# The recurrent layer's output projection by quarters: seven products of 512 x 512 x 512 in place of eight

## The chip, the cores and the metric

The program runs on one core of a Trainium2 chip. The metric is the device time of one execution in microseconds (us); less is better. Engines are called PE (matmul), PEld (its weight load), DVE (vector), ACT (scalar), POOL (GpSimd) and SP (the queue that issues the transfers).

## What is computed

A trunk of two layers over 1024 tokens behind 16 learned meta tokens, 1024 wide: attention first, then the recurrent layer that is changed here. In the recurrent layer every channel runs a linear recurrence over the tokens, its result is multiplied by a gate, and the product is projected and added to the residual; a last norm follows, and the 16 meta tokens are dropped.

```
h = rmsnorm(x, b_norm_g);  u, gate = split(h @ b_w_in)
uc = causal_conv4(u);  r, i = sigmoid(uc @ w_rg + b_rg), sigmoid(uc @ w_ig + b_ig)   # 4 blocks of 256
a = exp(-8 r softplus(-lam));  hs[t] = a[t] hs[t-1] + sqrt(1 - a^2) (i uc)
y = hs * silu(gate)
out = rmsnorm(x + y @ b_w_out, final_norm_g)[16:]
```

All is float32. Each matrix product is made of three matmuls: both operands are split into a rounded high part (ACT copies it, `hi_of`) and the remainder (DVE subtracts, `lo_of`), and high x high, high x low and low x high are added in one accumulating bank (`mm3`, lines 85 to 88).

## The kernel before

The recurrent layer works by channel tile: 8 tiles `ct` of 128 channels, in 4 blocks of two. `b_u(ct)` makes the convolved input `uc` (bank names `pu`; three multiply-adds on DVE, L768) and its split `uh`, `ul`. `b_rec(blk, us)` makes the two gates of a block (banks `pz`, 72 matmuls of 348 or 344 columns that read `uh`, `ul` of both tiles), then on ACT sigmoid, exp, tanh and square root, and on DVE the recurrence as a scan (L813). `b_gate(ct)` makes `silu(gate)` (banks `pg`, 2 x 24 matmuls of 512 columns, sigmoid on ACT, product on DVE at L834) and leaves it in `Y[:, ct]`. `b_mul(ct)` multiplies `Y` by the scan's result: on POOL, for the last tile on DVE (L822). The table `gates` says which gates stand ahead of which block.

The projection then takes the 8 token tiles of 128 in turn. For each it splits `Y` (`yh_b`, `yl_b`), and for both halves of 512 output columns adds 8 x 3 matmuls in a bank `bo`, so 384 in all; the last tile's second half is cut in two pieces of 256 columns, which makes 408. DVE adds the bank to the residual row `h` (L887), ACT squares it (L888), and the norm follows (`rms_r`, L132 to L140; result `ot`, L899), then the store. The weights `wb` come in through a pool of four stage buffers of 512 KB (tag `stg`) and are split like the rest (L572).

Each engine works through its own queue in order. The order in the queues is not that of the code alone: the framework's scheduler places instructions by an estimate of its own, so a later step's instruction can stand ahead of an earlier step's. PSUM has 8 banks here: six under tag `m` (`ps_m`) and two under tag `t` (`ps_t`).

Of the kernel before, what the change touches and what calls it, by code (L numbers as in the profile page):

```python
# [62 lines left out]
def trunk(ctx, tc, x, meta, a_norm_g, a_w_in, a_q_g, a_kv_g, a_w_uq, a_w_ukv, a_w_out,  # L63
# [799 lines left out]


    st_w2, pw2 = open_pool("wo2", bufs=1)
    st_bo, pbo = open_pool("bo", bufs=2, side="right")
    g_f = pbo.tile([P, D], F32, name="g_f", bufs=1)
    nc.sync.dma_start(g_f, final_g.rearrange("(a d) -> a d", a=1).broadcast_to([P, D]))
    wb0b = load_wo(pw2, b_w_out, 0, "wb", 6, (2, 3))
    ws = [(wb0[0] + wb0b[0], wb0[1] + wb0b[1]), load_wo(pw2, b_w_out, 1, "wb", 6)]  # L870
    for i in range(SEQ // P):
# [24 lines left out]
        for half in range(2):
            c = slice(half * 512, (half + 1) * 512)
            if not last:
                nc.vector.scalar_tensor_tensor(ot[:, c], ht[:, c], r, g_f[:, c], ALU.mult, ALU.mult)  # L899
            elif half:  # L900
                nc.vector.tensor_scalar(ot[:, c], ot[:, c], r, None, ALU.mult)
            else:
                nc.scalar.activation(ot[:, c], ot[:, c], AF.Copy, scale=r)
# [45 lines left out]
```

## Time and profile before

| | us |
|---|---|
| median of 3 runs (lowest, highest) | 934.7 (933.69, 935.65) |
| the profiled execution's own time | 937.55 |
| its span, first to last instruction | 935.7 |
| PE busy, DVE busy, ACT busy, POOL busy | 904.4, 554.3, 458.0, 35.6 |
| mean granted PE clock, of full | 0.99 |

The profile is one execution; its rows count from the span's start. Matmuls overlap, so the time that a row gives for one is longer than the step from one to the next; the step is read from starts. On DVE and ACT too the next instruction starts a little before the row of the one ahead ends.

### The profile page before, as it was taken

Reading aid. Unit: us, or ns where it says so; the run is one execution under the profiler, and the core shown is the slowest. Engines: PE = TensorE matmul, PEld = TensorE weight load, DVE = VectorE, ACT = ScalarE, POOL = GpSimd, SP = SyncE. Lnnn points to the kernel's source line nnn. Section 1 sums busy time; section 2 is a strip of 40 time slices with the busy share of each in tenths; the row PEclk is TensorE's granted clock in tenths of the full one; section 3 lists DMA queues with packets and bytes.
Section 4 is the critical chain, followed back from the end, with each engine's and each line's share of the span. In section 5 each row is a group of like instructions: output and inputs, shape, how many; then the busy total and the mean of one; then the engine's idle time right before and its main releaser. Section 6 shows DMA issues by size and latency. Waiting matters only on the chain.

```text
span 935.7 us, 13771 instructions
## 1 busy us (share of the span) xinstructions
PE 904.4 (97%) x5351; PEld 831.5 (89%) x5351; DVE 554.3 (59%) x1188; ACT 458.0 (49%) x937; POOL 35.6 (4%) x38
## 2 busy tenths in 40 slices
...
DMA packets 68449, 67.02 MB, mean 72 GB/s; under 512 B 14896, under 2 KB 52528, under 8 KB 68384
## 3 DMA queue, kind: packets, MB, share of 16 engines
...
## 4 chain that ended last, share of the span: by engine, by line
PE 87%; ACT 5%; DVE 5%; DMA 2%; issue 2%; SPq 0%; ACTq 0%; DVEq 0%
PE pt L536 4%; PE ga L87 3%; PE ga L86 3%; PE ga L88 3%; PE bo L87 3%; PE ao L86 3%; PE bo L88 3%; PE ao L88 3%; PE bo L86 3%; PE ao L87 3%; PE pu L88 2%; PE pu L86 2%; PE pu L87 2%; PE s L491 2%; PE o L88 2%; PE o L87 2%
## 5 line engine op out<-in xcount | busy, mean ns | idle before, releaser
L509 ACT ACTIVATE p<-s,m 116x116 f32<-116x116 f32 (+4 forms) x80 | 55.4, 694 | 42.8 <-PE pt L536 15.2
L80 ACT ACTIVATE pth<-pt 116x348 fp32r<-116x348 f32 (+5 forms) x152 | 57.7, 397 | 29.3 <-PE pt L536 25.6
L83 DVE TENSOR_TENSOR ptl<-pt,pth 116x348 fp32r<-116x348 f32 (+5 forms) x152 | 64.0, 437 | 10.3 <-ACT pth L80 9.7
L88 PE MATMUL pu<-x2h,l_wu 128*128 128x348 f32 (+1 forms) x192 | 61.5, 321 | 0.4 <-DVE l_wu L83 0.4
L88 PE MATMUL ga<-xth,l_wg 128*128 128x348 f32 (+1 forms) x192 | 61.7, 321 | 0.0
L86 PE MATMUL pu<-x2h,h_wu 128*128 128x348 f32 (+1 forms) x192 | 61.7, 322 | 0.0
L87 PE MATMUL pu<-x2l,h_wu 128*128 128x348 f32 (+1 forms) x192 | 61.7, 321 | 0.0
L87 PE MATMUL ga<-xtl,h_wg 128*128 128x348 f32 (+1 forms) x192 | 61.6, 321 | 0.0
L86 PE MATMUL ga<-xth,h_wg 128*128 128x348 f32 (+1 forms) x192 | 61.5, 320 | 0.0
L501 DVE CUSTOM_DVE_ANT_0 s<-s,maskt 116x116 f32<-116x116 f32 (+8 forms) x72 | 49.4, 686 | 17.6 <-PE s L495 17.6
L536 PE MATMUL pt<-ident,p 116*116 116x116 f32 (+1 forms) x360 | 54.6, 263 | 2.3 <-DVE ptl L83 1.8
L87 PE MATMUL bo<-wbl,yh_b 128*128 128x512 f32 (+1 forms) x136 | 51.9, 383 | 1.3 <-DVE wbl L572 1.3
L86 PE MATMUL bo<-wbh,yh_b 128*128 128x512 f32 (+1 forms) x136 | 51.8, 383 | 1.1 <-ACT wbh L80 1.1
L86 PE MATMUL ao<-wah,yh_a 128*128 128x512 f32 x128 | 50.5, 396 | 1.7 <-ACT yh_a L80 1.1
L88 PE MATMUL bo<-wbh,yl_b 128*128 128x512 f32 (+1 forms) x136 | 51.2, 380 | 0.0
L87 PE MATMUL pg<-x2l,h_wbg 128*128 128x512 f32 x128 | 50.6, 395 | 0.0
L88 PE MATMUL pg<-x2h,l_wbg 128*128 128x512 f32 x128 | 50.3, 393 | 0.0
L88 PE MATMUL ao<-wah,yl_a 128*128 128x512 f32 x128 | 50.3, 394 | 0.0
L86 PE MATMUL pg<-x2h,h_wbg 128*128 128x512 f32 x128 | 50.2, 392 | 0.0
L87 PE MATMUL ao<-wal,yh_a 128*128 128x512 f32 x128 | 49.8, 391 | 0.0
L491 PE MATMUL s<-kh,qh 128*116 128x348 f32 (+7 forms) x120 | 42.1, 351 | 6.7 <-ACT p L509 6.7
L536 PEld LDWEIGHTS pt<-ident,p 116*116 116x116 f32 (+1 forms) x360 | 41.5, 135 | 5.9 <-DVE ptl L83 2.5
...
## 6 DMA issues: line engine op xcount, KB each, us to landing
wg<-in_a_w_in SPq DMA_DIRECT2D x8, 512.0 KB, 3.9
wa<-in_a_w_out SPq DMA_DIRECT2D x8, 512.0 KB, 3.5
wu<-in_b_w_in SPq DMA_DIRECT2D x8, 512.0 KB, 4.0
wbg<-in_b_w_in SPq DMA_DIRECT2D x8, 512.0 KB, 3.9
wb<-in_b_w_out SPq DMA_DIRECT2D x8, 512.0 KB, 3.9
h<-hscr SPq DMA_DIRECT2D x8, 512.0 KB, 3.9
...
x<-in_x SPq DMA_DIRECT2D x7, 512.0 KB, 3.3
```

Source lines behind the costliest of these rows:

```text
L80: nc.scalar.activation(dst, src, AF.Copy)
L83: nc.vector.tensor_tensor(dst, src, bc(hi), ALU.subtract)
L86: nc.tensor.matmul(ps, lh, rh, start=start, stop=False)
L87: nc.tensor.matmul(ps, lh, rl, start=False, stop=False)
L88: nc.tensor.matmul(ps, ll, rh, start=False, stop=stop)
L491: nc.tensor.matmul(ps, a, kth[:, k0:k0 + w], start=True, stop=False)
L501: MKD[h, t] = nc.vector.tensor_tensor_reduce(pv, pv, mk, 1.0, -NEG, ALU.add, ALU.min, m[:, s:s + 1])
L509: MK[h, t] = nc.scalar.activation(dst, pv, AF.Exp, bias=mx, scale=-1.0, accum_out=l[:, s:s + 1])
L536: nc.tensor.transpose(pv[:nk, j], p[:, k0:k0 + nk], ident[:n, :n])
```

## The change

The projection of `Y` (1024 tokens x 1024 channels) by `b_w_out` is written as a product of 2 x 2 quarters of 512, with seven products of quarters in place of eight (Strassen's way, with 15 sums, in Winograd's form). `a11`, `a12` are the first 512 tokens with channel tiles 0 to 3 and 4 to 7, `a21`, `a22` the second 512 tokens.

- Each product is 4 banks (128 tokens each) x 4 channel tiles x 3 matmuls of 512 columns: 48, so 336 in all. The products run in the order P1, P7, P2, P6, P5, P3, P4 (each named by the numbers of its operands, `w1` and `y1` to `w7` and `y7`). Banks `b2` stay in use through P1, P7, P6 and P4, `b1` holds P2, `b3` holds P5 and P3; the partial sums in a bank are read between products.
- Sums of `Y` quarters are 4 DVE instructions of 2048 elements per partition (L976, L993, L1007, L1008), in place in `Y`. Each product's left operand is split anew: one ACT and one DVE instruction of 2048 (L893, L894), for P1 two of 1024.
- Sums of weights are made by the transfer: a plain load on SP, then a load from POOL's queue that adds to what lies in the stage buffer (`accum_op`, L872). There are eight of these, of 512 KB. `wchain` takes W12, then + W22, + W11, + W21, and is split in between for P7, P6 and P4; `wt1` is W11 + W12. Each weight operand is split as before, 7 x 2 instructions of 1024 on ACT and on DVE.
- All 8 residual rows are loaded ahead (`hr`), in the space that `x2h`, `x2l` had until the last gate; a finished bank is added to, or taken from, one or two quarters of them (`upd`, L949 and L951, 512 columns, 36 times in place of 17). Square, norm and store follow for each token tile (`square`, `finish`); the last tile is no longer cut.
- Gate 6 moves ahead of the last block's recurrence (`gates`), and gate 7 stands alone behind it.

The line numbers of the rows below in `order` fences that are above 840 are those of the changed kernel.

```diff
@@ -82,10 +82,10 @@
     def lo_of(dst, src, hi):
         nc.vector.tensor_tensor(dst, src, bc(hi), ALU.subtract)
 
-    def mm3(ps, lh, ll, rh, rl, start, stop):
-        nc.tensor.matmul(ps, lh, rh, start=start, stop=False)
-        nc.tensor.matmul(ps, lh, rl, start=False, stop=False)
-        nc.tensor.matmul(ps, ll, rh, start=False, stop=stop)
+    def mm3(ps, lh, ll, rh, rl, start, stop, **kw):
+        nc.tensor.matmul(ps, lh, rh, start=start, stop=False, **kw)
+        nc.tensor.matmul(ps, lh, rl, start=False, stop=False, **kw)
...
-    gates = {0: [0], 1: [1, 2], 2: [3, 4], 3: [5]}
+    gates = {0: [0], 1: [1, 2], 2: [3, 4], 3: [5, 6]}
...
-    wb0 = load_wo(pw1, b_w_out, 0, "wb", 2, (0, 1))
-    for ct in (6, 7):
-        b_gate(ct)
-        gated.add(ct)
-        settle()
...
+    TI = SEQ // (2 * P)
+    def w_raw(name):
+        return [stage(f"{name}_{j}").rearrange("p (k c) -> p k c", k=2) for j in range(2)]
+    def w_load(raw, kq, nq, add=False):
+        for j in range(2):
+            r0 = kq * 512 + j * 2 * P
+            src = b_w_out[r0:r0 + 2 * P, nq * 512:(nq + 1) * 512].rearrange("(k p) c -> p k c", p=P)
+            if add:
+                nc.gpsimd.dma_start(raw[j], src, accum_op=ALU.add)
+            else:
+                nc.sync.dma_start(raw[j], src)
+    def w_split(raw, pool, name):
+        th, tl = ("wh", "wl") if pool is wpg else ("woh", "wol")
+        hs, ls = [], []
+        for j in range(2):
+            hi = pool.tile([P, 2, 512], F32R, name=f"h_{name}_{j}", tag=th, bufs=2)
+            lo = pool.tile([P, 2, 512], F32R, name=f"l_{name}_{j}", tag=tl, bufs=2)
+            hi_of(hi, raw[j])
+            lo_of(lo, raw[j], hi)
+            hs.append(hi)
+            ls.append(lo)
+        return hs, ls
+    def yq(cq, tq, t0=0, n=512):
+        c0 = NMETA + tq * 512 + t0
+        return Y[:, 4 * cq:4 * cq + 4, c0:c0 + n]
+    def y_split(yv, yh, yl, sign):
+        nc.scalar.activation(yh, yv, AF.Copy, scale=float(sign))
+        nc.vector.scalar_tensor_tensor(yl, yv, float(sign), bc(yh), ALU.mult, ALU.subtract)
+    def product(banks, w, ys, first):
+        for i in range(TI):
+            yh, yl, o = ys(i)
+            for k in range(4):
+                mm3(banks[i], yh[:, k, o:o + P], yl[:, k, o:o + P], w[0][k // 2][:, k % 2], w[1][k // 2][:, k % 2],
+                    first and k == 0, k == 3, skip_group_check=True)
+    g7 = gate_w(KT - 1)
+    r1 = w_raw("wq11")
+    w_load(r1, 0, 0)
+    w1 = w_split(r1, pw1, "wq11")
+    ra = w_raw("wchain")
+    w_load(ra, 0, 1)
+    b_gate(KT - 1, g7)
+    gated.add(KT - 1)
+    settle()
+    y1 = []
+    for j in range(2):
+        yh = pbw.tile([P, 4, 256], F32R, name=f"y1h{j}", tag=("up", "uh")[j], bufs=2)
+        yl = pbw.tile([P, 4, 256], F32R, name=f"y1l{j}", tag=("up", "ul")[j], bufs=2)
+        y_split(yq(0, 0, 256 * j, 256), yh, yl, -1)
+        y1.append((yh, yl))
+    w_load(ra, 1, 1, True)
+    b2 = [ps_m(f"b2_{i}") for i in range(TI)]
+    product(b2, w1, lambda i: (*y1[i // 2], (i % 2) * P), True)
...
+    hr = []
+    for i in range(2 * TI):
+        h_ = pbo.tile([P, D], F32, name=f"hr{i}", tag="hr", bufs=2 * TI)
         t0 = NMETA + i * P
-        ys = [y_half(wpg if i == 0 else pbo, j, t0, P, f"b{i}", 2) for j in range(2)]
-        ht = pbo.tile([P, D], F32, name=f"h2_{i}", tag="ht", bufs=3)
-        nc.sync.dma_start(ht, hscr[t0:t0 + P, :])
-        ot = pbo.tile([P, D], F32, name=f"ot{i}", tag="ot", bufs=2)
-        last = i == SEQ // P - 1
-        cuts = (0, 512, 768, 1024) if last else (0, 512, 1024)
-        pieces = list(zip(cuts, cuts[1:]))
-        ms = sml.tile([P, 3], F32, name=f"fms{i}", tag="ms2")[:, :len(pieces)]
-        junk = wpg.tile([P, D], F32, name=f"junkf{i}", tag="wh") if last else ot
-        for j, (c0, c1) in enumerate(pieces):
-            half, o = c0 // 512, c0 % 512
-            ps = ps_m(f"bo{j}_{i}")[:, :c1 - c0]
-            out_mm(ps, ys, *[[w[:, :, o:o + c1 - c0] for w in ww] for ww in ws[half]])
-            hv = ht[:, c0:c1]
-            nc.vector.tensor_tensor(hv, ps, hv, ALU.add)
-            nc.scalar.activation(junk[:, c0:c1], hv, AF.Square, scale=1.0 / 32.0, accum_out=ms[:, j:j + 1])
-            if last:
-                nc.vector.tensor_tensor(ot[:, c0:c1], hv, g_f[:, c0:c1], ALU.mult)
+        nc.sync.dma_start(h_, hscr[t0:t0 + P, :])
+        hr.append(h_)
...
+    def yc(yv, name, sign=1):
+        yh = pbo.tile([P, 4, 512], F32R, name=f"ych_{name}", tag="ych", bufs=2)
+        yl = pbo.tile([P, 4, 512], F32R, name=f"ycl_{name}", tag="ycl", bufs=2)
+        y_split(yv, yh, yl, sign)
+        return lambda i: (yh, yl, i * P)
...
+    def upd(bank, i, cols, op):
+        h_ = hr[i][:, cols]
+        if op is ALU.add:
+            nc.vector.tensor_tensor(h_, bank, h_, ALU.add)
+        else:
+            nc.vector.tensor_tensor(h_, h_, bank, ALU.subtract)
...
+    a11, a12, a21, a22 = yq(0, 0), yq(1, 0), yq(0, 1), yq(1, 1)
+    w7 = w_split(ra, wpg, "wt3")
+    nc.vector.tensor_tensor(a21, a21, a11, ALU.subtract)
+    y7 = yc(a21, "s3")
+    for i in range(TI):
+        upd(b2[i], i, LEFT, ALU.subtract)
+        upd(b2[i], i, RIGHT, ALU.add)
+    r2 = w_raw("wq21")
+    w_load(r2, 1, 0)
+    w_load(ra, 0, 0, True)
+    product(b2, w7, y7, False)
+    g_f = pfo.tile([P, D], F32, name="g_f", bufs=1)
+    nc.sync.dma_start(g_f, final_g.rearrange("(a d) -> a d", a=1).broadcast_to([P, D]))
+    w2 = w_split(r2, pw1, "wq21")
+    y2 = yc(a12, "a12")
+    for i in range(TI):
+        upd(b2[i], i, RIGHT, ALU.subtract)
+    nc.vector.tensor_tensor(a21, a22, a21, ALU.subtract)
+    r5 = w_raw("wt1")
+    w_load(r5, 0, 0)
+    b1 = other("b1")
+    product(b1, w2, y2, True)
+    w6 = w_split(ra, wpg, "wt2")
+    y6 = yc(a21, "s2")
+    w_load(r5, 0, 1, True)
+    w_load(ra, 1, 0, True)
+    for i in range(TI):
+        upd(b1[i], i, LEFT, ALU.add)
+        square(i, 0) if i < 2 else None
+    nc.vector.tensor_tensor(a11, a11, a21, ALU.subtract)
+    nc.vector.tensor_tensor(a12, a12, a21, ALU.subtract)
+    product(b2, w6, y6, False)
+    w5 = w_split(r5, pw1, "wt1")
+    y5 = yc(a11, "s1")
+    r3 = w_raw("wq22")
+    w_load(r3, 1, 1)
+    for i in range(TI):
+        upd(b2[i], i, RIGHT, ALU.add)
+        upd(b2[i], i + TI, RIGHT, ALU.add)
+    b3 = other("b3")
+    product(b3, w5, y5, True)
+    w3 = w_split(r3, wpg, "wq22")
+    y3 = yc(a12, "s4")
+    for i in range(TI):
+        upd(b3[i], i + TI, RIGHT, ALU.add)
+    product(b3, w3, y3, False)
+    w4 = w_split(ra, pw1, "wt4")
+    y4 = yc(a22, "a22", -1)
+    for i in range(TI):
+        upd(b3[i], i, RIGHT, ALU.add)
+        if i >= 2:
+            square(i, 0)
+        square(i, 1)
+        finish(i)
+    product(b2, w4, y4, False)
+    for i in range(TI):
+        square(i + TI, 1)
+        upd(b2[i], i + TI, LEFT, ALU.subtract)
+        square(i + TI, 0)
+        finish(i + TI)
```

PE, where the last block's recurrence matmuls start (`pz6`, `pz7`: blocks' gates for channel tiles 6 and 7; `uh7`, `ul7`: the second tile's convolved input); before:

```order
L88 MATMUL pg5_1_8302<-x2h_6171,l_wbg5_8272 128x512
L86 MATMUL pz6_0_0_8339<-uh6_8170,h_wri3_8334 128x348
L87 MATMUL pz6_0_0_8339<-ul6_8171,h_wri3_8334 128x348
L88 MATMUL pz6_0_0_8339<-uh6_8170,l_wri3_8335 128x348
L86 MATMUL pz6_0_1_8347<-uh6_8170,h_wri3_8334 128x348
L87 MATMUL pz6_0_1_8347<-ul6_8171,h_wri3_8334 128x348
L88 MATMUL pz6_0_1_8347<-uh6_8170,l_wri3_8335 128x348
L86 MATMUL pz6_0_2_8355<-uh6_8170,h_wri3_8334 128x344
L87 MATMUL pz6_0_2_8355<-ul6_8171,h_wri3_8334 128x344
L86 MATMUL pz6_0_0_8339<-uh7_8265,h_wri3_8334 128x348
L86 MATMUL pz6_0_1_8347<-uh7_8265,h_wri3_8334 128x348
L88 MATMUL pz6_0_2_8355<-uh6_8170,l_wri3_8335 128x344
```

and with the change:

```order
L88 MATMUL pg6_1_8362<-x2h_6171,l_wbg6_8332 128x512
L86 MATMUL pz6_0_0_8399<-uh6_8170,h_wri3_8394 128x348
L87 MATMUL pz6_0_0_8399<-ul6_8171,h_wri3_8394 128x348
L88 MATMUL pz6_0_0_8399<-uh6_8170,l_wri3_8395 128x348
L86 MATMUL pz6_0_0_8399<-uh7_8265,h_wri3_8394 128x348
L87 MATMUL pz6_0_0_8399<-ul7_8266,h_wri3_8394 128x348
```

The 48 matmuls of gate 6 (`pg6`) now stand between gate 5 (`pg5`) and these; before, gate 5 was followed at once by the recurrence, and the first ones that read `uh7` came ninth and tenth.

DVE, behind the last block's first scan (`z6`, `z7`: recurrence; `pg7`: gate 7; `wb`: projection weights); before:

```order
L812 TENSOR_TENSOR z7_1_8413<-z7_0_8388,z7_1_8413 128x1040
L83 TENSOR_TENSOR yl_b0_0_8640<-Y_1217,yh_b0_0_8639 128x512
L834 TENSOR_TENSOR Y_1217<-pg6_1_8501,Y_1217 128x512
L813 SCALAR_TENSOR_TENSOR z7_0_8388<-a7_8441,z7_1_8413 128x1040
L834 TENSOR_TENSOR Y_1217<-pg7_0_8536,Y_1217 128x512
L822 TENSOR_TENSOR Y_1217<-Y_1217,z7_0_8388 128x512
L83 TENSOR_TENSOR yl_b0_1_8644<-Y_1217,yh_b0_1_8643 128x512
L834 TENSOR_TENSOR Y_1217<-pg7_1_8563,Y_1217 128x512
L822 TENSOR_TENSOR Y_1217<-Y_1217,z7_0_8388 128x512
L572 TENSOR_TENSOR wbl0_2_8606<-wb0_2_8603,wbh0_2_8605 128x1024
```

and with the change (`b2_0` to `b2_3`: the four banks of P1; `hr`: residual rows; `ycl_s3`: low part of P7's left operand; `wt3`, `wq21`: right operands of P7 and P2):

```order
L812 TENSOR_TENSOR z7_1_8473<-z7_0_8448,z7_1_8473 128x1040
L837 TENSOR_TENSOR Y_1217<-pg7_1_8567,Y_1217 128x512
L951 TENSOR_TENSOR hr0_8667<-hr0_8667,b2_0_8606 128x512
L949 TENSOR_TENSOR hr0_8667<-b2_0_8606,hr0_8667 128x512
L894 SCALAR_TENSOR_TENSOR ycl_s3_8693<-Y_1217,ych_s3_8692 128x2048
L813 SCALAR_TENSOR_TENSOR z7_0_8448<-a7_8501,z7_1_8473 128x1040
L951 TENSOR_TENSOR hr1_8669<-hr1_8669,b2_1_8607 128x512
L949 TENSOR_TENSOR hr1_8669<-b2_1_8607,hr1_8669 128x512
L951 TENSOR_TENSOR hr2_8671<-hr2_8671,b2_2_8608 128x512
L949 TENSOR_TENSOR hr2_8671<-b2_2_8608,hr2_8671 128x512
L822 TENSOR_TENSOR Y_1217<-Y_1217,z7_0_8448 128x512 x2
L83 TENSOR_TENSOR l_wq21_0_8761<-wq21_0_8704,h_wq21_0_8760 128x1024
```

The reading of P1's banks, P7's operand and P2's weights now share DVE's queue with the second scan; behind these rows stand one more bank's update, the sum at L993 and the low part of P2's left operand (`ycl_a12`), of 2048 elements.

DVE at the end of the program; before, the last rows but the norm of the last tile:

```order
L140 SCALAR_TENSOR_TENSOR r_f6_9188<-r_f6_9188,t_f6_9189 128x1
L899 SCALAR_TENSOR_TENSOR ot6_9129<-h2_6_9127,r_f6_9188,g_f_8601 128x512 x2
L887 TENSOR_TENSOR h2_7_9207<-bo0_7_9212,h2_7_9207 128x512
L890 TENSOR_TENSOR ot7_9209<-h2_7_9207,g_f_8601 128x512
L887 TENSOR_TENSOR h2_7_9207<-bo1_7_9240,h2_7_9207 128x256
L890 TENSOR_TENSOR ot7_9209<-h2_7_9207,g_f_8601 128x256
L892 TENSOR_TENSOR fmt7_9296<-fms7_9210 128x1
L887 TENSOR_TENSOR h2_7_9207<-bo2_7_9268,h2_7_9207 128x256
L890 TENSOR_TENSOR ot7_9209<-h2_7_9207,g_f_8601 128x256
```

and with the change, from the third of the last product's four tiles:

```order
L951 TENSOR_TENSOR hr6_8679<-hr6_8679,b2_2_8608 128x512
L951 TENSOR_TENSOR hr7_8681<-hr7_8681,b2_3_8609 128x512
L966 TENSOR_TENSOR fmt4_9184<-fms4_9179 128x1
L133 TENSOR_SCALAR v_f4_9186<-fmt4_9184 128x1
L134 RECIPROCAL t_f4_9188<-t_f4_9188 128x1
L136 SCALAR_TENSOR_TENSOR r_f4_9187<-t_f4_9188,v_f4_9186 128x1
L966 TENSOR_TENSOR fmt5_9203<-fms5_9198 128x1
L140 SCALAR_TENSOR_TENSOR r_f4_9187<-r_f4_9187,t_f4_9188 128x1
L133 TENSOR_SCALAR v_f5_9205<-fmt5_9203 128x1
L970 SCALAR_TENSOR_TENSOR ot4_9180<-hr4_8675,r_f4_9187,g_f_8758 128x512 x2
```

Before, each tile's norm and output stand behind that tile's own bank. With the change both last banks' updates (`hr6`, `hr7`) stand ahead of the norm and output of token tiles 4 to 7, of which tile 4's are shown and the other three follow in the same way.

## Rows read from the trace of the kernel before

**Rows 1.** The page, part 1: busy time, share of the span, instructions.

```profile
PE 904.4 (97%) x5351; PEld 831.5 (89%) x5351; DVE 554.3 (59%) x1188; ACT 458.0 (49%) x937; POOL 35.6 (4%) x38
```

**Rows 2.** Busy time by stretch; the first row names the columns.

```profile
core 0: us, PE busy (x) PEld busy (x) DVE busy (x) ACT busy (x) POOL busy (x), PEclk, DMA share, GB/s
740.00:760.00 20.00, 20.00 (x104) 17.72 (x104) 8.26 (x9) 8.69 (x14) 2.69 (x3) 1.00 0.18 56
797.09:814.46 17.37, 14.65 (x74) 13.90 (x72) 7.89 (x7) 8.86 (x15) 2.56 (x2) 0.80 0.15 52
814.46:836.70 22.24, 22.24 (x99) 18.03 (x97) 14.53 (x13) 13.91 (x15) 4.20 (x2) 1.00 0.21 71
836.70:847.34 10.64, 8.31 (x29) 6.14 (x28) 9.79 (x13) 6.98 (x10) 1.18 (x1) 0.84 0.50 167
847.34:928.78 81.44, 81.40 (x382) 68.22 (x380) 37.13 (x83) 22.72 (x52) 0.00 (x0) 1.00 0.24 82
928.78:935.70 6.92, 0.00 (x0) 0.00 (x0) 2.19 (x8) 1.52 (x4) 0.00 (x0) 0.68 0.20 76
```

**Rows 3.** Timeline of PE, last block's recurrence: start, length, instruction, [idle before].

```profile
800.67 0.59 PE L86 MATMUL pz<-uh,h_wri 128*128 128x348 f32 x2 [2.17 <-ACT uh L80]
...
802.63 0.66 PE L87 MATMUL pz<-ul,h_wri 128*128 128x348 f32 x1 [0.56 <-DVE ul L83]
...
805.11 0.49 PE L87 MATMUL pz<-ul,h_wri 128*128 128x348 f32 x1
805.40 0.49 PE L88 MATMUL pz<-uh,l_wri 128*128 128x348 f32 x1
...
808.28 0.37 PE L86 MATMUL pz<-uh,h_wri 128*128 128x344 f32 x1
```

**Rows 4.** Timeline of PE, start of the projection.

```profile
840.66 0.50 PE L86 MATMUL bo<-wbh,yh_b 128*128 128x512 f32 x1 [1.07 <-ACT wbh L80]
842.42 0.75 PE L87 MATMUL bo<-wbl,yh_b 128*128 128x512 f32 x1 [1.26 <-DVE wbl L572]
```

**Rows 5.** Timeline of ACT, the first gate sigmoid behind the last block's square roots.

```profile
826.29 0.60 ACT L308 ACTIVATE Y<-pg 128x512 f32<-128x512 f32 x1
```

**Rows 6.** Groups by form, 780 to 936: count, busy us, mean ns, idle before.

```profile
L822 POOL TENSOR_TENSOR Y<-Y,z 128x512 f32<-128x512 f32 x6 | 12.3, 2060 | 78.2 <-DVE z L813 59.8 <-DVE Y L834 18.4
...
L887 DVE TENSOR_TENSOR h<-bo,h 128x512 f32<-128x512 f32 x15 | 10.4, 690 | 21.4 <-PE bo L88 17.3 <-issue 4.1
...
L813 DVE TENSOR_TENSOR_SCAN z<-a,z 128x1040 f32<-128x1040 f32 x4 | 9.3, 2316 | 0.1
...
L572 DVE TENSOR_TENSOR wbl<-wb,wbh 128x1024 fp32r<-128x1024 f32 x6 | 7.0, 1219 | 1.2 <-ACT wbh L80 1.2
...
L80 ACT ACTIVATE wbh<-wb 128x1024 fp32r<-128x1024 f32 x6 | 5.9, 1044 | 0.0
...
L812 DVE TENSOR_TENSOR z<-z,z 128x1040 f32<-128x1040 f32 x3 | 3.7, 1220 | 0.0
```

**Rows 7.** Timelines of POOL and DVE, where both work and where DVE works alone.

```profile
781.57 4.38 POOL L822 TENSOR_TENSOR Y<-Y,z 128x512 f32<-128x512 f32 x2 [34.22 <-DVE z L813]
...
782.48 2.32 DVE L83 TENSOR_TENSOR l_wbg<-wbg,h_wbg 128x1024 fp32r<-128x1024 f32 x1
...
841.15 4.62 DVE L572 TENSOR_TENSOR wbl<-wb,wbh 128x1024 fp32r<-128x1024 f32 x4
```

**Rows 8.** Timelines of DVE and SP's queue, the last two tiles' norms.

```profile
919.07 0.16 DVE L892 TENSOR_TENSOR fmt<-fms 128x1 f32<-128x1 f32 x1 [0.79 <-ACT ot L888]
...
920.24 1.41 DVE L899 SCALAR_TENSOR_TENSOR ot<-h,r_f,g_f 128x512 f32<-128x512 f32 x2
...
930.95 0.49 DVE L901 TENSOR_SCALAR ot<-ot,r_f 128x512 f32<-128x512 f32 x1
```

**Rows 9.** Transfers: count, KB each, median us from issue to landing.

```profile
wb<-in_b_w_out SPq DMA_DIRECT2D x8, 512.0 KB, 3.9
...
csk<-in_rope_k SPq DMA_DIRECT2D x1, 288.0 KB, 7.4
```

More of the change, by code (lines that the diff above doesn't have):

```diff
@@ L83, in lo_of @@
         nc.vector.tensor_tensor(dst, src, bc(hi), ALU.subtract)
-    def mm3(ps, lh, ll, rh, rl, start, stop):
-        nc.tensor.matmul(ps, lh, rh, start=start, stop=False)
-        nc.tensor.matmul(ps, lh, rl, start=False, stop=False)
-        nc.tensor.matmul(ps, ll, rh, start=False, stop=stop)
+    def mm3(ps, lh, ll, rh, rl, start, stop, **kw):
+        nc.tensor.matmul(ps, lh, rh, start=start, stop=False, **kw)
+        nc.tensor.matmul(ps, lh, rl, start=False, stop=False, **kw)
+        nc.tensor.matmul(ps, ll, rh, start=False, stop=stop, **kw)
     def mm_stack(ps, xp, k, n, wh, wl):
@@ L822, in b_mul, with gate_w, b_gate @@
             (nc.vector if ct == KT - 1 else nc.gpsimd).tensor_tensor(yv, yv, r[:, c0:c0 + 512], ALU.mult)
-    def b_gate(ct):
+    def gate_w(ct):
         raw = load_wcols(b_w_in, D + ct * P, KT, P, f"wbg{ct}")
-        wh, wl = split_page(raw, [P, KT, P], f"wbg{ct}")
+        return split_page(raw, [P, KT, P], f"wbg{ct}")
+    def b_gate(ct, pages=None):
+        wh, wl = pages or gate_w(ct)
         for c in range(2):
@@ L862, in trunk @@
     st_x2.close()
[L865 to L871, printed above, removed]
-        t0 = NMETA + i * P
-        ys = [y_half(wpg if i == 0 else pbo, j, t0, P, f"b{i}", 2) for j in range(2)]
-        ht = pbo.tile([P, D], F32, name=f"h2_{i}", tag="ht", bufs=3)
-        nc.sync.dma_start(ht, hscr[t0:t0 + P, :])
-        ot = pbo.tile([P, D], F32, name=f"ot{i}", tag="ot", bufs=2)
-        last = i == SEQ // P - 1
-        cuts = (0, 512, 768, 1024) if last else (0, 512, 1024)
-        pieces = list(zip(cuts, cuts[1:]))
-        ms = sml.tile([P, 3], F32, name=f"fms{i}", tag="ms2")[:, :len(pieces)]
-        junk = wpg.tile([P, D], F32, name=f"junkf{i}", tag="wh") if last else ot
-        for j, (c0, c1) in enumerate(pieces):
-            half, o = c0 // 512, c0 % 512
-            ps = ps_m(f"bo{j}_{i}")[:, :c1 - c0]
-            out_mm(ps, ys, *[[w[:, :, o:o + c1 - c0] for w in ww] for ww in ws[half]])
-            hv = ht[:, c0:c1]
-            nc.vector.tensor_tensor(hv, ps, hv, ALU.add)
-            nc.scalar.activation(junk[:, c0:c1], hv, AF.Square, scale=1.0 / 32.0, accum_out=ms[:, j:j + 1])
-            if last:
-                nc.vector.tensor_tensor(ot[:, c0:c1], hv, g_f[:, c0:c1], ALU.mult)
@@ new lines, in trunk @@
+    st_bo, pbo = open_pool("bo", bufs=2)
+    st_fo, pfo = open_pool("fo", bufs=2, side="right")
+    hr = []
+    for i in range(2 * TI):
+        h_ = pbo.tile([P, D], F32, name=f"hr{i}", tag="hr", bufs=2 * TI)
+        t0 = NMETA + i * P
+        nc.sync.dma_start(h_, hscr[t0:t0 + P, :])
[5 more added lines that the diff above has]
+        return lambda i: (yh, yl, i * P)
@@ new lines, in other, with square @@
+    def other(name):
+        return [(ps_m if i < 2 else ps_t)(f"{name}_{i}") for i in range(TI)]
+    LEFT, RIGHT = slice(0, 512), slice(512, 1024)
+    def upd(bank, i, cols, op):
[4 more added lines that the diff above has]
+            nc.vector.tensor_tensor(h_, h_, bank, ALU.subtract)
+    fms, junks = {}, {}
+    def square(i, half):
+        if i not in fms:
+            fms[i] = sml.tile([P, 2], F32, name=f"fms{i}", tag="ms2", bufs=2 * TI)
+            junks[i] = pfo.tile([P, D], F32, name=f"ot{i}", tag="ot", bufs=2)
+        c = slice(half * 512, half * 512 + 512)
+        nc.scalar.activation(junks[i][:, c], hr[i][:, c], AF.Square, scale=1.0 / 32.0,
+                             accum_out=fms[i][:, half:half + 1])
@@ L891, in trunk, with finish @@
+    def finish(i):
+        ot = junks[i]
         mt = sml.tile([P, 1], F32, name=f"fmt{i}", tag="ms")
-        nc.vector.tensor_tensor(mt, ms[:, 0:1], ms[:, 1:2], ALU.add)
-        if last:
-            nc.vector.tensor_tensor(mt, mt, ms[:, 2:3], ALU.add)
+        nc.vector.tensor_tensor(mt, fms[i][:, 0:1], fms[i][:, 1:2], ALU.add)
         r, _ = rms_r(mt, P, 1, f"f{i}")
```

10 lines of the change are left out of this document (2 added, 8 removed).

## The prediction

> **What bounds the kernel now.** I read the page's busy times first, then busy time by stretch over the last 140 us, then the timelines of the stretches in which PE was not busy, last the groups by form for prices. PE is busy 97% of the span and DVE 59% [rows 1], so work taken from PE pays at once as long as DVE, ACT and the transfers keep up, and PE's idle time is the other thing to look for. From 797 to the end there are three places of it [rows 2]. The last block's recurrence takes 17.37 us with PE busy for 14.65 at a granted clock of 0.80. The projection's first 10.64 us have 8.31 busy, clock 0.84. Behind the last matmul come 6.92 us of norm and store. The rest is packed: both gates (96 matmuls) take 22.24 us, 11.12 each, and the projection's main part 81.44 us for 332 matmuls of 512 columns and 48 of 256, as many columns as 356: 0.228 us for 512. All prices below are from this one execution; its own time is 937.55 for a span of 935.7, the median 934.7, and the sum is taken off each alike.
>
> **The recurrence: minus 6.0.** The ninth matmul waited 2.17 us for the copy of `uh7`, a later one 0.56 for `ul7` [rows 3]. After the first wait PE went at the lower of its two levels (1.2 GHz): steps of 0.29 us for 348 columns against (814.46 - 808.28) / 39 = 0.158 from 808.28 on [rows 2, 3]. Undisturbed, 72 matmuls take 11.3, so 6.0 are lost. With the change gate 6 stands in front, 11.12 us of PE work, and `uh7`, `ul7` are wanted only at 797.09 + 11.12 = 808.2. DVE has more to do before that: one stage slot serves gate 5's weights, `wq11_0` and `wq11_1` in turn. Gate 5's split ends at 784.80 [rows 7], a load lands 3.9 later [rows 9], copy and split take 1.04 and 1.22 [rows 6]: 791.2. One more multiply-add (1.2, as the 1040-wide rows), three ACT copies in a row (3.1) and a split bring gate 6's weights to about 796.8, just in time for 797.1; two more multiply-adds and splits bring `ul7` to 805 or 806. I take the whole 6.0; a load that lands later would take up to 1.5 of it. So the recurrence ends at 819.5, gate 7 at 830.7, where P1 starts (the old projection started at 836.7).
>
> **The matmuls: minus 11.2; the old start: minus 4.2.** 336 at 0.228 is 76.6. The old projection lasted 836.70 to 928.78, 92.08 us. In its first 10.64, 28 matmuls at 0.228 would have taken 6.4; the other 4.2 are two waits for weight splits (1.07 and 1.26) and the lower clock after them [rows 2, 4]. So 87.8 becomes 76.6, and the 4.2 go, since P1's weights and both its operands come early.
>
> **DVE at the start of the products: plus 4.6, and 1.0 for the clock.** The first sigmoid of the last gate ended 12.3 us behind the recurrence's last matmul (826.29 + 0.60 against 814.6) [rows 2, 5]; ACT now has one 1.0 us copy more in that chain, so it ends at 819.5 + 12.3 + 1.0, about 832.9. From there DVE's queue to the low part of P2's operand holds: 13 instructions of 512, 2 of 1040, 3 splits of 1024, 2 scans, 3 of 2048. Four splits in a row took 4.62, a step of 1.155, 0.065 under the mean of one [rows 6, 7]; I take that off each row: 13 x 0.62 + 2 x 1.155 + 3 x 1.155 + 2 x 2.25 + 3 x 2.2 = 25. The 2.2 is an estimate: 0.690 for 512 and 1.219 for 1024 [rows 6] make 2.28 for 2048 on a line. One of these meets tile 6's product on POOL, where a DVE instruction on two SBUF tiles took 2.32 instead of 1.22 [rows 7]: 1.1 more. Sum 26.1, done at 859.0. PE in that time has P1, three banks of P7, eight matmuls of P2 and P7's last bank: 104 x 0.228 = 23.7, done at 854.4. It waits 4.6 us in all, ahead of P7's first bank (low part, about 844.7), its second bank (two updates), and P2's remainder. Bounds: 3.5 without POOL, 8 if all three large ones are slowed. Waits of this size lowered the clock twice [rows 3, 4]; but while DVE is what PE waits for, a slower PE costs little, so 1.0, between 0 and rival A's 8.
>
> Behind that DVE just keeps up. During the rest of P2 and the first eight matmuls of P6 (48 x 0.228 = 10.9) it has three updates, two sums, a split and a low part, 9.6; for P5 and P3 about 9.5 and 9.4 against 10.9. The sum at L976 goes into DVE's queue two blocks earlier, where DVE is busy 8.26 us of 20 [rows 2]; without that gap it would cost its 2.2.
>
> **The transfers: 0.** No row shows an accumulating load. The nearest are plain ones: 3.9 us for 512 KB, at worst 7.4 for 288 KB in small pieces [rows 9]; I take 5, since these rows are 2 KB long like those of `wb`. The first is issued near 802.5 (gate 6's split, then a plain load) and wanted by ACT at 820.4, 18 us later; the tightest, `wt1`, near 855.5 (P2's split, then a plain load) and wanted at 866, when P2's reads release the split's buffers. Both ends fit. The rows `hr` start when gate 7 ends; even one after the other, `hr3` would land at 830.7 + 4 x 3.9 = 846.3, and is used at 852.
>
> The trace shows DVE and POOL slowing each other where both work, not one shut out [rows 7]. The Trainium skill's page SBUF — State Buffer, section SBUF: two separate sides, warns that a transfer issued by GpSimd starves while DVE holds their shared port, since GpSimd can't write its descriptors. That speaks against this change; its list names copies in the two-port mode, and its section Who interferes with whom leaves tensor-tensor work out, by inference. No row here shows it; by it the transfers would start late, which is rival B's case, near 935, and by the rows the sum stays.
>
> **The end: plus 8.0.** Before, only one tile's norm was left behind the last matmul. Now the updates of the last two banks stand ahead of the norms of tiles 4 to 7 on DVE, so four norms start when PE ends. One took 919.07 to 921.65, 2.58 with ACT's square root in between [rows 8]. One update 0.62, 4 x 2.58 = 10.3, and from the last DVE instruction (930.95 + 0.49) to the span's end 4.2, of which ACT's parallel half was done 0.2 later: 4.0. That is 14.9 against 6.92 [rows 2]; bounds 13.5 and 16.
>
> **The sum.** -6.0 - 11.2 - 4.2 + 4.6 + 1.0 + 8.0 = -7.8. Span 927.9, that execution 929.7, median 926.9.
>
> **The rivals.**
> A, the clock stays low through P7. Four waits within 15 us; the lower level lasted 7.6 us after 2.17 of idling [rows 3]. At 0.228 x 0.29 / 0.158 = 0.42, the 54 matmuls from 844.8 on take 22.6 and end at 867.4 instead of 859.0: 8.4, so 934. If P2's other 40 are slow too, 942. Against it: between the waits PE works without a gap, and the clock came back in such work.
> B, the other side: accumulating loads are slow, or begin late. Let one take T. The first holds up ACT's queue, and all behind it, by T - 18; `wt1` then holds up P5 by T - 10.5 - 3 (its split has about 3 to spare). At T = 20 that is 2 + 6.5, and the gain is gone; at 25 it is 18.5: 945. Against it: T would have to be 2.7 times the slowest load shown. For it: nothing here shows one.
> C, DVE is late in every product. Its rows add to some 72 us beside 76.6 of PE before the end, and P6 has 1.3 of margin. If one of 2048 takes 2.6, or POOL's transfers slow it as its products do, P2, P6 and the end lose 4 more: 931.
> D, less is lost: DVE's work of 2048 costs less than the line says and ACT's early squares let the last norms close up: waits 2, end 13, clock 0, so 922.
>
> **How the numbers follow.** Forecast 0.54 (its own range 924 to 930), A 0.13, B 0.11, C 0.14, D 0.08. 922 to 935 leaves out the slow ends of A and B and little below. About 0.2%, 1.9 us, can be told from no change here. Faster are the forecast, C, D and a little of A and B: 0.80. Same: the near ends of A and B, 0.07. Slower: their far ends, 0.13.
>
> **What would show it.** In the changed profile: no wait ahead of the first `pz` reading `uh7`, and 72 of them in about 11.4 us; P1 starting near 831; waits of PE between 841 and 860 ended by DVE (`ycl_s3`, `hr`, `ycl_a12`), some 5 us; no wait ended by a transfer of POOL's queue; about 15 us between PE's last matmul and the end, with DVE busy most of it. The forecast is wrong if loads of `wchain` or `wt1` end waits of ACT, if the clock's digit stays under 9 beyond one slice, or if PE waits for DVE after 870.

## The result, and the profile after

The changed kernel takes 928.6 us (median of 4 runs, 928.06 to 929.28); the kernel before, on the same chip, 934.3 (median of 4). The ratio is 0.9937, with a 95% interval of 0.992 to 0.9955: 5.9 us less, at least 4.2 and at most 7.5. The forecast was 926.9, its range 922 to 935. The profiled execution has an own time of 928.06 and a span of 926.3.

The page's first part, to be set against [rows 1]:

```profile
PE 888.9 (96%) x5279; PEld 816.0 (88%) x5279; DVE 584.7 (63%) x1206; ACT 466.3 (50%) x932; POOL 43.6 (5%) x46
```

PE has 15.5 us less, DVE 30 us more. Busy time by stretch shows where it went. The cuts are gates 5 and 6, the last block's recurrence, gate 7, P1, from P1's end to just behind P2's wait, the rest of the products, and what follows the last matmul:

```profile
core 0: us, PE busy (x) PEld busy (x) DVE busy (x) ACT busy (x) POOL busy (x), PEclk, DMA share, GB/s
784.65:806.89 22.24, 22.24 (x98) 18.03 (x97) 19.42 (x16) 11.73 (x15) 4.59 (x4) 1.00 0.50 122
806.89:818.27 11.38, 11.38 (x74) 11.38 (x72) 3.07 (x3) 7.66 (x14) 0.53 (x1) 1.00 0.23 86
818.27:829.41 11.14, 11.14 (x50) 9.02 (x49) 4.36 (x4) 11.08 (x11) 1.20 (x1) 1.00 0.29 49
829.41:840.58 11.17, 11.17 (x50) 9.01 (x48) 10.77 (x13) 6.19 (x7) 4.65 (x3) 1.00 0.87 314
840.58:858.81 18.23, 15.77 (x67) 11.97 (x65) 18.23 (x18) 6.91 (x5) 2.39 (x2) 1.00 0.71 188
858.81:910.34 51.53, 51.53 (x224) 41.69 (x222) 43.93 (x66) 19.91 (x31) 2.39 (x2) 1.00 0.34 88
910.34:926.30 15.96, 0.00 (x0) 0.00 (x0) 9.42 (x29) 5.87 (x20) 0.00 (x0) 0.66 0.38 140
```

The recurrence went from 17.37 us [rows 2] to 11.38, without a wait and at the full clock. The products take 80.93 from P1's start to the last matmul's end, against 92.08 for the projection before. The stretch behind the last matmul has grown from 6.92 to 15.96, and DVE is busy for only 9.42 of it. The products' PE waits are three, all of them ended by DVE (timeline of PE):

```profile
842.32 0.50 PE L88 MATMUL b<-h_wt,ycl_s 128*128 128x512 f32 x1 [1.12 <-DVE ycl_s L894]
845.74 0.50 PE L86 MATMUL b<-h_wt,ych_s 128*128 128x512 f32 x1 [0.81 <-DVE hr L949]
856.61 0.51 PE L88 MATMUL b<-h_wq,ycl_a 128*128 128x512 f32 x1 [0.53 <-DVE ycl_a L894]
```

They stand at the three places that the prediction named: P7's first bank, its second bank, and P2's remainder, and they add to 2.46 us. DVE in the same time (its timeline) has no idle time in any row:

```profile
839.43 2.84 DVE L894 SCALAR_TENSOR_TENSOR ycl_s<-Y,ych_s 128x2048 fp32r<-128x2048 f32 x1
842.19 2.31 DVE L813 TENSOR_TENSOR_SCAN z<-a,z 128x1040 f32<-128x1040 f32 x1
844.42 0.66 DVE L951 TENSOR_TENSOR hr<-hr,b 128x512 f32<-128x512 f32 x1
845.00 0.68 DVE L949 TENSOR_TENSOR hr<-b,hr 128x512 f32<-128x512 f32 x1
...
852.07 2.28 DVE L993 TENSOR_TENSOR Y<-Y 128x2048 f32<-128x2048 f32 x1
854.27 2.28 DVE L894 SCALAR_TENSOR_TENSOR ycl_a<-Y,ych_a 128x2048 fp32r<-128x2048 f32 x1
```

P7's low part ends at 842.3, where PE starts again; the second scan comes between it and the updates of P1's second bank, for which PE waits next.

Behind the last matmul, the timeline of ACT (squares L960, square roots L132) shows a wait that the prediction didn't have:

```profile
909.80 0.63 ACT L960 ACTIVATE ot<-hr 128x512 f32<-128x512 f32 x1 [4.58 <-DVE hr L951]
...
911.28 0.63 ACT L960 ACTIVATE ot<-hr 128x512 f32<-128x512 f32 x1
...
916.70 0.63 ACT L960 ACTIVATE ot<-hr 128x512 f32<-128x512 f32 x1 [3.38 <-DMA out_h<-ot]
```

The last of these is the first square of token tile 6. What it squares had been complete for long, since the right half of that tile is finished before the last product. It waits for a store: the thrown-away squares go into `ot`, which has two buffers, so tile 6 can't be squared until tile 4's output has landed. The row at 909.80 is tile 4's first square, which waits for tile 2's stores in the same way (the last of them landed at 909.70), though the profile puts it down to a DVE instruction that ended at the same time.

DVE's timeline over the same time, the last update and the starts of the norms of tiles 4 and 6:

```profile
910.37 0.69 DVE L951 TENSOR_TENSOR hr<-hr,b 128x512 f32<-128x512 f32 x1 [0.68 <-PE b L88]
911.17 0.16 DVE L966 TENSOR_TENSOR fmt<-fms 128x1 f32<-128x1 f32 x1
...
918.06 0.16 DVE L966 TENSOR_TENSOR fmt<-fms 128x1 f32<-128x1 f32 x1 [1.54 <-ACT ot L960]
```

Tile 4's norm starts behind the last update, in the order that the prediction read; tile 6's starts 1.54 us late, for its squares.

### The profile page after: what moved, and what is told of

It reads as the page before. It is cut to its first block, busy times and chain, and to the rows that moved or that the text cites. A ratio compares the mean times of both kernels' runs of the same rounds, so it can differ in the third digit from the quotient of the medians.

```text
span 926.3 us, 13669 instructions
## 1 busy us (share of the span) xinstructions
PE 888.9 (96%) x5279; PEld 816.0 (88%) x5279; DVE 584.7 (63%) x1206; ACT 466.3 (50%) x932; POOL 43.6 (5%) x46
## 4 chain that ended last, share of the span: by engine, by line
PE 89%; DVE 4%; ACT 3%; DMA 3%; issue 1%; SPq 1%; DVEq 0%; ACTq 0%
PE pt L536 4%; PE pu L88 3%; PE ga L86 3%; PE pu L86 3%; PE ga L87 3%; PE ga L88 3%; PE pu L87 3%; PE pg L87 3%; PE pg L88 3%; PE pg L86 3%; PE ao L86 3%; PE ao L88 3%; PE ao L87 3%; PE s L491 2%; PE o L88 2%; PE o L87 2%
## 5 line engine op out<-in xcount | busy, mean ns | idle before, releaser
L83 DVE TENSOR_TENSOR ptl<-pt,pth 116x348 fp32r<-116x348 f32 (+5 forms) x152 | 64.0, 437 | 10.3 <-ACT pth L80 9.6
L87 PE MATMUL o<-ptl,v 116*128 116x348 f32 (+1 forms) x144 | 45.1, 313 | 0.0
L88 PE MATMUL o<-pth,v 116*128 116x348 f32 (+1 forms) x144 | 43.9, 305 | 0.0
L86 PE MATMUL o<-pth,v 116*128 116x348 f32 (+1 forms) x144 | 43.0, 298 | 0.0
```

The source lines that it names most:

```text
L83: nc.vector.tensor_tensor(dst, src, bc(hi), ALU.subtract)
L86: nc.tensor.matmul(ps, lh, rh, start=start, stop=False, **kw)
L87: nc.tensor.matmul(ps, lh, rl, start=False, stop=False, **kw)
L88: nc.tensor.matmul(ps, ll, rh, start=False, stop=stop, **kw)
```

## The experiments

Each profile was cut at fixed points of the program: gate 5's first matmul, the recurrence, gate 7, the first product or projection matmul, the last matmul, the end. This matters, because gate 5, ahead of which the kernels barely differ, starts at 784.4 to 789.0 from one execution to the next.

**The kernel before, again.**

> The kernel before, profiled a second time, with nothing changed. The profile that the sum was made against lies 3.2 us above the median (own time 937.55 against 934.31). Theory one (as the prediction took it): the surplus is spread over the whole span, so the last block's recurrence again takes about 17.4 us, the projection with its first stalls about 92.1 and the tail about 6.9. Theory two: the surplus sits in the stalls of the first profile; then the second profile's span is near 932.5 and one of these three stretches is 1 to 3 us shorter.

Own time 937.0, span 935.2, beside a median of 936.3 for this kernel's other runs on the same chip. By stretch (gate 5, recurrence, gates 6 and 7, projection, end):

```profile
786.66:797.78 11.12, 11.12 (x50) 9.02 (x49) 9.74 (x7) 4.51 (x5) 0.66 (x1) 1.00 0.14 47
797.78:813.95 16.17, 13.32 (x73) 12.63 (x72) 8.54 (x8) 9.41 (x16) 2.57 (x2) 0.89 0.20 66
813.95:836.19 22.24, 22.24 (x98) 18.03 (x97) 14.52 (x13) 13.91 (x15) 4.20 (x2) 1.00 0.21 71
836.19:928.21 92.02, 89.69 (x409) 74.33 (x407) 46.92 (x94) 29.70 (x62) 1.19 (x1) 0.98 0.27 92
928.21:935.20 6.99, 0.00 (x1) 0.00 (x0) 2.19 (x8) 1.53 (x4) 0.00 (x0) 0.76 0.20 75
```

Neither theory holds whole. The projection and the end are the same to 0.1 us; the recurrence is 1.2 shorter, since PE idled 2.85 us in one piece and the clock was low for less of it (0.89 against 0.80 in [rows 2]). From gate 5 on the first profile took 149.7, this one 148.5, and the changed kernel 141.65: 8.1 or 6.9 less. The rest of the difference between the two shown spans, 9.4 us, is a start of gate 5 at 785.97 against 784.65.

**Gate 6 ahead, with the old projection.**

```diff
-    gates = {0: [0], 1: [1, 2], 2: [3, 4], 3: [5]}
+    gates = {0: [0], 1: [1, 2], 2: [3, 4], 3: [5, 6]}
...
-    for ct in (6, 7):
+    for ct in (7,):
```

> The kernel before with one edit: gate 6 stands ahead of the last block's recurrence, gate 7 alone behind it; the projection keeps its eight products. Theory one (the prediction's term of minus 6.0 stands by itself): the recurrence takes 11.4 us in place of 17.4 and the time is 928.3. Theory two (the move pays only because P1 and P7 need nothing of the last block): in the kernel before, the last tile of Y was complete 26.8 us after the recurrence's last matmul, and 22.24 us of gates lay over that; with gate 7 alone 11.1 are left, so the projection starts 11 us earlier but waits up to 11 us longer for Y and its weights; time 932 to 939, with the recurrence itself still at 11.4 us.

Slower than before: 940.4 us, ratio 1.0053 (1.0035 to 1.007). The stretches of the recurrence and of the projection's start, and a row of PE's timeline in the latter:

```profile
808.03:819.34 11.31, 11.31 (x73) 11.30 (x72) 3.07 (x3) 7.46 (x13) 0.00 (x0) 1.00 0.14 46
...
830.46:845.33 14.87, 4.18 (x16) 2.96 (x15) 14.45 (x13) 6.20 (x8) 4.32 (x2) 0.78 0.15 51
```
```profile
844.53 0.80 PE L87 MATMUL bo<-wbl,yh_b 128*128 128x512 f32 x1 [9.31 <-DVE wbl L572]
```

Theory two, just over its upper end (1.0053 of 934.3 is 939.3). The recurrence lost its stall as the prediction said, but the old projection, now behind one gate instead of two, idles 10.7 us in its first 14.87: the weight split that it waits for is done at 844.5, no earlier than before (842.4 in [rows 4]). Gate 6 had covered that time. So the 6.0 us are no gain of that move alone; they are one because P1 and P7 read only the first four channel tiles and fill the time.

**Seven products, gate 6 put back.**

```diff
-    gates = {0: [0], 1: [1, 2], 2: [3, 4], 3: [5, 6]}
+    gates = {0: [0], 1: [1, 2], 2: [3, 4], 3: [5]}
...
+    b_gate(6)
+    gated.add(6)
+    settle()
     g7 = gate_w(KT - 1)
```

> The changed kernel with gate 6 put back behind the last block's recurrence, the seven products as they are. Theory one (the terms add): the stall at the second tile's split returns, plus 6.0, but P1 starts 11 us later against the recurrence's chain on ACT and DVE, so the waits of 2.5 us at P7 and P2 go: 932. Theory two (the stall was one execution's own, not the order's): 927 to 929, with the recurrence at 11.4 to 14 us in the profile.

933.6 us, ratio 0.9978 (0.9965 to 0.999), 0.0041 above the changed kernel's: theory one. The recurrence and the products:

```profile
797.57:815.71 18.14, 13.30 (x74) 12.79 (x73) 10.94 (x9) 9.59 (x17) 5.08 (x4) 0.91 0.58 134
...
837.97:915.63 77.66, 77.66 (x337) 62.89 (x335) 65.37 (x88) 31.20 (x41) 7.60 (x6) 1.00 0.52 148
```

The stall is back (6.8 us more than 11.38), and with the later start not one wait is left in the products. So 336 matmuls take 77.66 here, and in the changed kernel DVE's lateness costs 80.93 - 77.66 = 3.3 us. That is more than the 2.46 of its three waits: idle time is counted from the end of a matmul's row, some 0.16 us after the next one could have started, and the first step behind each wait is 0.34 us in place of 0.23.

**Eight buffers of `ot`.**

```diff
-            junks[i] = pfo.tile([P, D], F32, name=f"ot{i}", tag="ot", bufs=2)
+            junks[i] = pfo.tile([P, D], F32, name=f"ot{i}", tag="ot", bufs=8)
```

> The changed kernel with eight buffers in place of two for the tile ot, which takes the squares that are thrown away, and then the output; nothing else is edited. Theory one (the two buffers set the end: a square waits until an earlier tile's store has landed): the squares run as the banks come, the stretch behind the last matmul falls from 16.0 us to about 10 and the time to 922 to 924. Theory two (the prediction's: the order on DVE sets the end, four norms in a row behind the last two updates, whatever the buffers): the stretch stays at 15 to 16 us and the time at 928.6.

923.8 us, ratio 0.9877 (0.9856 to 0.9898): 5.6 us under the changed kernel by the ratios. Its products and its end:

```profile
831.98:912.91 80.93, 78.41 (x337) 62.67 (x335) 75.32 (x110) 38.14 (x59) 9.44 (x7) 1.00 0.51 146
912.91:922.10 9.19, 0.00 (x0) 0.00 (x0) 5.66 (x15) 1.02 (x3) 0.00 (x0) 0.64 0.55 206
```

The end fell by 6.8 us, and the products take the same 80.93: theory one. In DVE's queue the norms of tiles 4 and 5 now stand ahead of the last update (its timeline; the first row is tile 5's output, the second the last update):

```profile
912.51 1.42 DVE L970 SCALAR_TENSOR_TENSOR ot<-hr,r_f,g_f 128x512 f32<-128x512 f32 x2
913.84 0.68 DVE L951 TENSOR_TENSOR hr<-hr,b 128x512 f32<-128x512 f32 x1
```

So the order on which the prediction built its tail followed from the two buffers. How much of the 6.8 us is this order and how much the waits that are gone isn't separated, since both changed together.

**Squares in a tile of their own.**

```diff
-        nc.scalar.activation(junks[i][:, c], hr[i][:, c], AF.Square, ...
+        jk = pfo.tile([P, 512], F32, name=f"jk{i}_{half}", tag="jk", bufs=2)
+        nc.scalar.activation(jk, hr[i][:, c], AF.Square, ...
```

> The changed kernel in which the thrown-away squares go to a tile of their own; ot keeps its two buffers. Theory one (what costs the time is the square's wait for the store of an earlier tile's ot): the stretch behind the last matmul falls to 9 to 10 us as with eight buffers, since the outputs themselves come 2.5 us apart and a store takes 2.1. Theory two (it is the number of outputs under way): 13 to 16 us.

921.9 us, ratio 0.9849 (0.983 to 0.9869); `ot` still has two buffers.

```profile
910.07:919.60 9.53, 0.00 (x0) 0.00 (x0) 6.09 (x17) 1.02 (x3) 0.00 (x0) 0.74 0.54 198
```

Theory one: taking the squares out of `ot` gives all of it but 0.3 us, with no more buffers for the outputs. Here too the order on DVE changed with it: tile 4's output stands ahead of the last update.

**Plain loads, and each addition twice.** In the first, `accum_op` is left out; in the second, the accumulating line stands twice.

> The changed kernel with the eight accumulating loads made plain loads on the same queue; the sums of weights are left out. Theory one (the transfers are hidden, cost 0): the time stays within 0.3% of 928.6, though a plain load lands in 3.5 to 4 us and an accumulating one in 5.8 to 6.3 alone. Theory two (the accumulation delays a wait somewhere that the chain does not name): 1 to 4 us less.

> The changed kernel with each accumulating load issued twice, so that the second addition begins when the first is done or shares the engines with it; the sums hold the added weights twice. Rival B's break-even is put to the test: the prediction gave the first sum 18 us of room and wt1 about 10.5, with a gain gone at 20 us. Theory one (room as worked out): a pair takes 11 to 14 us, the waits that appear are those of wt1 for P5 and perhaps of wchain for P4, and the time is 928.6 to 932. Theory two (the additions lie on the path already): plus 6 us or more for each link of the chain, over 940.

929.3 and 929.8 us, ratios 0.9927 (0.9902 to 0.9952) and 0.9929 (0.9905 to 0.9952): both as the changed kernel. From the first product to the last matmul they take 80.93 and 80.92:

```profile
833.80:914.73 80.93, 78.45 (x337) 62.67 (x335) 73.04 (x95) 33.01 (x43) 7.08 (x7) 1.00 0.39 142
```
```profile
831.36:912.28 80.92, 78.41 (x337) 62.67 (x335) 72.94 (x95) 33.24 (x43) 15.54 (x12) 1.00 0.72 180
```

The additions cost nothing. With each of them doubled, ACT's copies do wait for `wt1` (the view of waits, second kernel; longest 6.9 us), as theory one said, but PE still doesn't:

```profile
ACT h_wt L80 <- DMA wt<-in_b_w_out: 7.3, 2, 6.9
POOL wt L873 <- DMA wt<-in_b_w_out: 4.8, 2, 2.6
```

The two pairs for `wt1` had landed 11.8 and 12.8 us after the first load of each was issued, so they were inside the prediction's room of 10.5 + 3 us. That room is borne out up to there; where it ends wasn't tried.

**Less work on DVE at P7 and P2.** The updates of the right half behind P1 and P7 are left out:

```diff
-        upd(b2[i], i, RIGHT, ALU.add)
     r2 = w_raw("wq21")
...
-    for i in range(TI):
-        upd(b2[i], i, RIGHT, ALU.subtract)
```

> The changed kernel without the eight updates of the right half that read P1's banks and, behind P7, the same banks again (eight DVE instructions of 512 columns, some 4.8 us); the right half of the first 512 tokens is left out of the result in that part. Theory one (DVE's late queue makes the waits ahead of P7's second bank and P2's remainder): PE's idle time between 838 and 858, 2.5 us, falls under 1.3, and the time by 1 to 2 us. Theory two (the residual rows' loads, the last of which lands 12.6 us after its issue, or the scan make these waits): PE's idle time stays at 2 us or more and the time within 0.5 us.

927.7 us, ratio 0.9907 (0.9883 to 0.9932); by the runs alone this can't be told from the changed kernel, by the stretch it can: 79.50 us in place of 80.93, with one wait of PE left.

```profile
832.15:911.65 79.50, 78.15 (x337) 62.73 (x335) 68.97 (x87) 32.92 (x43) 11.57 (x7) 1.00 0.51 144
```
```profile
847.83 0.50 PE L86 MATMUL b<-h_wt,ych_s 128*128 128x512 f32 x1 [1.35 <-DVE hr L951]
```

Theory one, though the idle time left, 1.35 us, is just over the 1.3 that it allowed: eight instructions fewer took 1.4 of the 3.3 us. The wait that is left is that for the second bank, behind the scan.

**Left operands in halves of 256 tokens.** `yc` makes two tiles of 256 tokens instead of one of 512, for the six products from P7 on.

> The changed kernel with every left operand from P7 on split in two halves of 256 tokens, so that the first two banks wait only for the first half. Theory one (PE waits at P7 and at P2 for the whole of a low part): the waits of 1.12 us and 0.53 us go, DVE pays 0.06 us for each of six more instructions, and the time falls by 1 to 1.7 us. Theory two (DVE's total work up to P2's operand is the limit): the idle time moves on to the next update, and the time is the same within 0.5 us.

926.3 us, ratio 0.9896 (0.9872 to 0.992). The products, the end, and PE's waits:

```profile
829.19:909.38 80.19, 78.16 (x337) 62.73 (x335) 74.22 (x107) 35.24 (x53) 10.41 (x7) 1.00 0.50 145
909.38:923.00 13.62, 0.00 (x1) 0.00 (x0) 8.63 (x24) 4.89 (x15) 0.00 (x0) 0.62 0.42 154
```
```profile
841.07 0.47 PE L86 MATMUL b<-h_wt,ych_s 128*128 128x512 f32 x1 [0.56 <-DVE hr L958]
845.53 0.50 PE L86 MATMUL b<-h_wt,ych_s 128*128 128x512 f32 x1 [1.47 <-DVE hr L958]
```

The time fell, but by more than theory one's 1.7 us (3.1 from gate 5 on) and for another reason: the products gave 0.7 us, since PE's wait moved on to the updates (theory two), and 2.3 came at the end, where the framework's scheduler had made another order. By its total alone the run would have been taken for the wrong theory.

**Three edits together, and the last tile.** `combo` has the squares apart, four buffers of `ot`, and the halves; `combo_last` also multiplies the last tile by the norm's weights ahead of its factor.

> The changed kernel with three edits together: squares to a tile of their own, four buffers of ot, and left operands in halves of 256 tokens. Halves alone took 0.7 us from the products and 2.3 from the tail, eight buffers 6.8 from the tail. Theory one (the tail's gain is the same one in both): 7.0 to 7.6 us below the changed kernel, ratio to before 0.985 to 0.987. Theory two (they add): 9 to 10 us below, ratio 0.983.

> As combo, and the last tile's output is multiplied by the norm's weights ahead of its row factor, so that behind the factor ACT and DVE scale one half each. Theory one (the last tile's two 0.7 us products follow its factor on the path): the tail is 0.7 to 1 us shorter than combo's. Theory two (the two more DVE instructions stand ahead of the last factor and take it back): the same within 0.3 us.

923.5 and 923.0 us, ratios 0.9864 (0.9847 to 0.9881) and 0.986 (0.9842 to 0.9878). Products and end of the first, end of the second:

```profile
832.29:912.49 80.20, 78.15 (x337) 62.73 (x335) 75.38 (x112) 38.80 (x65) 10.41 (x7) 1.00 0.51 147
912.49:921.80 9.31, 0.00 (x0) 0.00 (x0) 5.97 (x18) 1.02 (x3) 0.00 (x0) 0.65 0.56 208
```
```profile
912.70:922.90 10.20, 0.00 (x0) 0.00 (x0) 6.25 (x19) 1.74 (x4) 0.00 (x0) 0.68 0.51 190
```

Theory one for the first: the tail's gain is one and the same. From gate 5 on `combo` takes 134.3 us, 7.4 less than the changed kernel, and `junk_apart` 135.2; their times can't be told apart. For the second neither theory holds: its end is 0.9 us longer, since its two additional products stood ahead of the last factor on DVE.

**The changed kernel, again.**

> The changed kernel again, beside those below. From gate 5's first matmul to the end the two profiles of the kernel before took 149.7 and 148.5 us, the changed one 141.7. Theory one (the rest of the span differs from execution to execution and has nothing to do with the change): gate 5 starts anywhere between 784.4 and 789.0, and from there to the end it is 141.7 again; the ratio to before lies at 0.991 to 0.995. Theory two (the changed kernel is also quicker ahead of gate 5): gate 5 starts at 784.7 again.

930.3 us beside 936.3 for the kernel before on that chip, ratio 0.9935 (0.9913 to 0.9956). Gate 5 started at 787.5; from there it took 141.7 us again, 80.91 and 16.02 of them in products and end. Theory one.

## Why the prediction was right, step by step

| term | predicted | measured, from gate 5 on | from |
|---|---|---|---|
| recurrence | -6.0 | -6.0 (second profile of before: -4.8) | 11.38 against 17.37 and 16.17 |
| matmuls | -11.2 | -10.1 | 77.66 in place of 76.6, against 87.8 |
| old start of the projection | -4.2 | -4.2 | no wait ahead of or in P1 |
| DVE late at P7 and P2 | +4.6 | +3.3 | 80.93 - 77.66 |
| clock | +1.0 | 0 | 1.00 in every stretch up to the last matmul |
| transfers | 0 | 0 | plain loads: 80.93 as well |
| end | +8.0 | +9.0 | 15.96 against 6.92 |
| sum | -7.8 | -8.0 | 149.7 to 141.65: -8.1 |

The sum came out nearer than its terms: four of them are off by 1.0 to 1.3 us, two each way, and that they cancel to 0.2 is luck.

**The recurrence** went as worked out: `uh7` and `ul7` were there in time, and 72 matmuls took 11.38 against 11.3. What the step left open is that this term hangs on the others. `gate6_alone` has it in full and is slower than before.

**The matmuls** were under-priced by 1.1 us. The step of 0.228 was the old projection's mean, rounded down from 0.2288 (0.3 us of the 1.1). It mixed two forms: the old 512-column matmuls came 0.227 us apart (54.40 us for 240, from 852.11), the last 48, of 256 columns, 0.120. In the change four of the seven products run at 0.233 (P1: 11.17 us for 48) and three at 0.227; the gates of the kernel before, 22.24 us for 96 [rows 2], had already shown a step of 0.232.

**DVE** had just the queue that was written down. From the end of the gate's first sigmoid (an ACT row, 830.73 + 0.60) to the end of P2's low part (856.55) it took 25.2 us, against 26.1; the 2048-wide instruction took 2.28, as the line through 512 and 1024 gave. Meeting POOL's product cost the one low part 0.56 (2.84 in place of 2.28), not 1.1. `no_right` and `halves` show that the waits are those of a full queue: taking work out shortens them, splitting an operand moves them. The 1.0 for the clock, which the prediction took from the waits in [rows 3] and [rows 4], wasn't lost; why the clock held isn't shown.

**The end** is the step that was read only in part. Its order came as predicted: behind the last update, four norms in a row on DVE. What its sum of 14.9 lacked is a wait: from 911.17 to the end of the last output at 923.14 the four norms took 12.0 us and not 10.3, because DVE idled 1.54 for tile 6's squares, which waited for tile 4's store. Behind the last DVE row came 3.2 us in place of 4.0, so part of the miss cancelled, and the total of 16.0 is at the upper bound. The larger thing it left open is why the order was so. The prediction took it as given and didn't ask which buffer a square's result goes into; with a buffer of its own for that result (`junk_apart`) 6.4 us go, the order on DVE with them. The kernel before had the same two buffers of `ot` for squares and outputs, but its token tiles ended some 10 us apart, so a store had landed long before its buffer was wanted again.

**The transfers** were hidden, and rival B is out. With no other beside it an accumulating load took 5.85 us to land, those that overlapped another one 5.6 to 7.8, and one beside the eight loads of `hr` 10.8, against 3.4 to 5.1 for plain ones on SP's queue other than `hr`. Two were issued while DVE was busy without a gap (18.23 of 18.23 us), at 853.37 and 855.61; they landed in 5.6 and 7.8 us. The first took no longer than the one of 5.85, for most of which DVE was idle; the second had the first beside it. The Trainium skill's page SBUF — State Buffer, section SBUF: two separate sides, has GpSimd's transfers starve while DVE holds their shared port. The trace shows none of that beside DVE's tensor-tensor and scalar-tensor-tensor work, which agrees with the page: its warning there names only the two-port mode. Rivals A and C didn't come either: the clock stayed at 1.00, and PE didn't wait between 858.81 and the last matmul.

**The step from the sum to the median** was the weak one beside the end. The prediction took 7.8 off the median as it stood. The first profile of before had the longer of the two stalls that were seen, 1.2 us over the second; with that one the sum is -6.9, and the measured ratio (4.2 to 7.5 us less) holds it. The median measured is 1.7 us over the forecast.
